# Adding three units' results to an SBUF residual with accumulating DMA transfers instead of VectorE

## The chip, the cores and the metric

The kernel runs on one core of a Trainium2 chip. Its time is the device time of one execution in microseconds; for the kernel before it is 1980.69 us, the median of two runs (1980.49 and 1980.89). A separate, profiled execution supplies the trace. All times inside the kernel are microseconds from the start of that trace's span, unless they are marked ns.

## The reference

One layer of an encoder block on 256 tokens of 2048 channels, all in float32:

```python
for l in range(DEPTH):                       # DEPTH = 1
    x = x + 0.5 * swiglu(rmsnorm(x, ffn1_norm[l]), ffn1_w_gate[l], ffn1_w_up[l], ffn1_w_down[l])
    h = rmsnorm(x, mix_norm[l])
    z = h @ w_in[l]                          # u, v and the gate logits
    ...                                      # a = pooling branch of u, b = convolution branch of v
    x = x + (g_a * a + g_b * b) @ w_out[l]
    x = x + 0.5 * swiglu(rmsnorm(x, ffn2_norm[l]), ffn2_w_gate[l], ffn2_w_up[l], ffn2_w_down[l])
return rmsnorm(x, final_norm)
```

`swiglu(h) = (silu(h @ w_gate) * (h @ w_up)) @ w_down` has a hidden width of 5632. The three assignments to `x` are the residual additions; the change concerns how they are carried out.

## The kernel before

**Tokens, units and chunks.** The 256 tokens are two token tiles of 128 partitions (t = 0, 1). The residual lies in SBUF for the whole run as two tiles `X[0]` and `X[1]`, 128 by 2048 float32 each. All weights stream from HBM once, as row tiles of 128 by 1024 float32 (512 KB). A *unit* is one product of the tokens with 1024 weight columns; a *chunk* is two row tiles of a unit. Each unit accumulates into one PSUM tile per token tile, `acc[t]`, of two banks of 512 columns. The pool of these tiles, `ps_a`, has three, so a new unit takes over the accumulators of the unit before it.

**The split.** Each row tile is turned into a rounded part `wh` (a cast on ScalarE, line 135) and a remainder `wl` (a subtraction on VectorE, line 137). Every product is three matmuls: high by high, high by low, low by high (line 208). The pool of split tiles holds two chunks, so the cast for a chunk waits until TensorE has finished the chunk two before it; five raw row tiles can be in SBUF, and SyncE issues a load when VectorE has finished with the tile in that place.

**The order of work.** The kernel is written out by hand: there is no scheduler, and each engine takes its instructions in the order in which the program emits them. For chunk i, `run` emits in this order: the load of a later chunk, the split of chunk i + 1, the functions that `at(i, ...)` has left for this place, and the matmuls of chunk i. When the last chunk of a unit has been emitted, the unit's `done` function follows. In that last chunk the matmuls of token tile 0 all come before those of token tile 1.

**What stands around the additions.** Five units add to the residual by the functions in question: the two halves of the first feed-forward's down product (`down_done`), the two halves of the mixer's output product (`wo_done`), and the first half of the second feed-forward's down product (`down_done` again). The second half of that last product ends in `final_tail`, which is not touched. With n for the last chunk of such a unit, each `done` does, for each token tile:

- two additions on VectorE, of 512 columns each, that read `acc` in PSUM and read and write `X` (line 301, with the factor 0.5; line 633 without one);
- `squares` (line 263): for each 512 columns of `X`, a ScalarE instruction with squared output and the row's sum, and one that reads the accumulator out.

For the first four of the five, `next_operand` then leaves work for later chunks. Before the matmuls of chunk n + 2, and again before those of n + 3, eight TensorE transposes read 512 columns of `X` (line 250; the first two groups q = 0, 1, then q = 2, 3). A group of four fills one of the two banks of `ps_t`, and ScalarE (line 241) and VectorE (line 242) turn it into the high and low part of the next product's operand. After a second half, `finish_rstd` is left for chunk n + 1: two small VectorE instructions on the sums of squares and a power on GpSimd (line 270).

The staging pool `stg` has two buffers for each tag; the tag `h` serves tiles of 128 by 512 float32. GpSimd's queue carries, besides that power, seven loads of broadcast rows (line 573).

Of the kernel before, what the change touches and what calls it, by code (L numbers as in the profile page):

```python
# [13 lines left out]
P = 128  # L14
# [20 lines left out]
WARM = 9  # L35
# after these row tiles of weights, the row tiles of x^T that are loaded
XT_LOADS = {(0, 0): (1, 2), (0, 1): (2, 4), (1, 0): (4, 8), (2, 0): (8, 12), (3, 0): (12, 16)}
TAPS = 6
TAPS_BUSY = 4

# columns of the packed per-partition vectors
V_N1, V_NM, V_N2 = 0, KD, 2 * KD
# [8 lines left out]
class Unit:  # L51
    """x[T, K*128] @ w[K*128, 1024]: K row tiles, two banks of 512 columns for each token tile."""

# [5 lines left out]
class Special:  # L59
    """A chunk of the weight stream with a use of its own."""  # L60

# [5 lines left out]
def encoder_kernel(ctx: ExitStack, tc: tile.TileContext, x, xT, vecs, rows, pool_m,  # L67
# [11 lines left out]

    # ---------------------------------------------------------------- constants and small state  # L80
    ident = const.tile([P, P], F32, name="ident")
# [10 lines left out]

    # ---------------------------------------------------------------- the stream of weight chunks
    stream = []
    side, middle = {}, {}

    def at(i, fn):
        """fn is emitted before the products of chunk i."""
        side.setdefault(i, []).append(fn)

    def amid(i, fn):
        """fn is emitted between the products of chunk i."""
        while isinstance(stream[i][0], Special):
            i += 1
        middle.setdefault(i, []).append(fn)
# [63 lines left out]
    def run_chunk(i):  # L169
        u, cc = stream[i]  # L170
        if isinstance(u, Special):
            u.use(split.pop(i))
            return
        if cc == 0:
            n = NT + 1 if u.tail else NT
            u.acc = [ps_a.tile([P, 2, C], F32, tag="acc", name=f"acc{i}_{t}") for t in range(n)]
        ws = split.pop(i)
        left = u.k // 2 - 1 - cc
        if u.tail and left < 2:
            # the last two chunks: token tile 0, then token tile 1 by columns  # L180
            for kk in range(2):
                products(u, 2 * cc + kk, 0, ws[kk])
            if left:
                u.kept = ws
                return
            u.tail(0, (0, 1), u.acc[0])
            for c in range(2):
                for kk in range(4):
                    products(u, 2 * cc - 2 + kk, 1, (u.kept + ws)[kk], (c,))
                u.tail(1, (c,), u.acc[1 + c])  # L190
            return
        order = [(kk, t) for kk in range(2) for t in range(NT)]
        if not left:
            order.sort(key=lambda o: o[1])
        for n, (kk, t) in enumerate(order):
            if n == 2:
                for fn in middle.pop(i, []):
                    fn()
            products(u, 2 * cc + kk, t, ws[kk])
        if not left:  # L200
            u.done(u.acc)
# [13 lines left out]

    # ---------------------------------------------------------------- operands of the products
    def pair(pool, tag, n, name):
        """hi and lo by row tile, four row tiles to a block."""
        r = []
        for b in range(n // 4):  # L220
            h, l = (block(pool, f"{tag}{s}{b}", F32R, f"{name}{s}{b}") for s in "hl")
            r += [(h[:, q, :], l[:, q, :]) for q in range(4)]
        return r
# [4 lines left out]
    def hidden(pool, name):  # L228
        """The feed-forward's hidden layer, hi and lo by row tile, four of them in a block."""
        return [tuple(block(pool, f"h{s}{u}", F32R, f"{name}{s}{u}") for s in "hl") for u in range(FF // C)]  # L230
# [7 lines left out]
    def scaled_split(dst, src, gain):  # L238
        """dst = hi and lo of src * gain, a scalar of each partition."""
        h, l = dst  # L240
        nc.scalar.activation(h, src, AF.Copy, scale=gain)
        nc.vector.scalar_tensor_tensor(out=l, in0=src, scalar=gain, in1=h.bitcast(F32),  # L242
                                       op0=ALU.mult, op1=ALU.subtract)

    def transposes(src_of, n, name):
        """n (up to 4 / NT) tiles [T, 128] into one bank as [128, T] each."""
        b = bank(name)
        for j in range(n):
            for t in range(NT):
                nc.tensor.transpose(out=b[:, j * T + t * P: j * T + (t + 1) * P],  # L250
                                    in_=src_of(j, t), identity=ident)
        return b

    def x_transposed(dst, gain_base, k0):
        """dst[k0], dst[k0 + 1] = the transposed residual times the gain."""
        b = transposes(lambda j, t: X[t][:, (k0 + j) * P:(k0 + j + 1) * P], 2, f"xt{Pos.now}_{k0}")
        for j in range(2):
            scaled_split(dst[k0 + j], b[:, j * T:(j + 1) * T], vcol(gain_base, k0 + j))

    def squares(t, slot, c0, c1):  # L260
        for n, c in enumerate(range(c0, c1, C)):
            junk = stg.tile([P, C], F32, tag="sg", name=f"sq{Pos.now}_{t}_{c}")
            nc.scalar.activation(junk, X[t][:, c:c + C], AF.Square,
                                 accum_out=ss[:, t, slot + n:slot + n + 1])

    def finish_rstd(dst):
        nc.vector.tensor_reduce(out=msq, in_=ss, axis=mybir.AxisListType.X, op=ALU.add)
        nc.vector.tensor_scalar(out=msq, in0=msq, scalar1=1.0 / D, scalar2=EPS,
                                op0=ALU.mult, op1=ALU.add)
        nc.gpsimd.tensor_tensor(dst, msq, mhalf, op=ALU.pow)  # L270

    # ---------------------------------------------------------------- feed-forward
    def ffn_units(w_g, w_d, xt, ht, rs, residual_done, tail=None):
# [22 lines left out]
        def down_done(half):  # L296
            def done(acc):
                for t in range(NT):
                    for c in range(2):
                        xs = X[t][:, half * W2 + c * C: half * W2 + (c + 1) * C]  # L300
                        nc.vector.scalar_tensor_tensor(out=xs, in0=acc[t][:, c, :], scalar=0.5, in1=xs,
                                                       op0=ALU.mult, op1=ALU.add)
                    squares(t, 2 * half, half * W2, (half + 1) * W2)
                residual_done(half)
            return done
# [6 lines left out]
    def next_operand(xt, gain_base, rs):  # L312
        """After each half of the residual: its transposed tiles, and in the end the row norms."""
        def f(half):
# [6 lines left out]

    # ---------------------------------------------------------------- pass 0: what starts the stream
    xt1 = pair(xtp, "x", KD, "xt1")
# [20 lines left out]

    # ---------------------------------------------------------------- plan
    def run(first, last):
# [9 lines left out]

    # phase 1
    ht_stack = ExitStack()
# [5 lines left out]

    # phase 2 units are appended before phase 1 runs, so that the weights run ahead
    mix = {}
# [62 lines left out]
    def ln_mean():  # L429
        """LayerNorm over the channels (partitions and tiles), spread over the chunks from here."""  # L430
        cv, cp = mix["conv"], conv_pairs()
# [93 lines left out]
    def use_pool_m(ws):  # L525
        """pooled^T = u^T M^T, M the window's sum less count times the token itself."""
        def group(g):
# [98 lines left out]
    def wo_done(half):  # L626
        def done(acc):
            if half == 0:
                xt3.extend(pair(xtp, "x", KD, "xt3"))
            for t in range(NT):  # L630
                for c in range(2):
                    xs = X[t][:, half * W2 + c * C: half * W2 + (c + 1) * C]
                    nc.vector.tensor_tensor(out=xs, in0=acc[t][:, c, :], in1=xs, op=ALU.add)
                squares(t, 2 * half, half * W2, (half + 1) * W2)
            next_operand(xt3, V_N2, rstd[2])(half)
# [18 lines left out]

    # phase 3 units
    ht2 = []
    fin = {}

    def final_tail(t, cs, acc):
        """The last of the residual, its norm and what is stored, for columns cs of token tile t."""  # L660
        pieces = [(c, 0, C) for c in cs] if t == 0 else [(c, a, T) for c in cs for a in (0, T)]
# [35 lines left out]

    # ---------------------------------------------------------------- run
    xr = [block(htp, f"h{s}{FF // C - 1 - j}", F32, f"xr{s}{j}") for j in range(2) for s in "hl"]
# [44 lines left out]
def _pack(w, cols):  # L744
    """[K*128, N] -> [units, K, 128, 1024]: cols[u] lists the column ranges of unit u."""
    import numpy as np
# [9 lines left out]
def _pool_constants():  # L756
    """M^T by window (tokens on partitions), and one over the counts."""
    import numpy as np
# [68 lines left out]
```

## Time and profile before

| what | value |
|---|---|
| median of the runs | 1980.69 us |
| span of the profiled execution, which is all that its record gives of its own time | 1978.6 us |
| runs' median less that span | 2.1 us |
| TensorE busy (matmul rows) | 1966.4 us, 99% |
| VectorE busy | 1110.4 us, 56% |
| ScalarE busy | 874.5 us, 44% |
| GpSimd busy | 11.0 us, 1% |
| mean granted TensorE clock | 0.999 |
| VectorE additions at line 301 / line 633 | 12 / 8 |

A busy share is a mean over stages. The view of chains follows the work that ended last back to what released each step; the timeline gives the instructions of a stretch in order of time, neighbours of one kind merged, with an idle time in brackets and what ended it.

### The profile page before, as it was taken

What the parts mean: (1) busy time and instruction counts of PE and PEld (TensorE: products, weight loads), DVE (VectorE), ACT (ScalarE), POOL (GpSimd) and SP (SyncE); (2) the same over time, 40 slices, a digit from 0 to 9 for tenths busy, and PEclk for the clock granted to TensorE, in tenths of its full rate; (3) what the DMA queues carried; (4) which work ended last, traced back from release to release, by engine and by line L of the source; (5) the groups of instructions that cost most, each with busy time, mean ns of one, the idle gap of its engine ahead of it and who ended that gap; (6) DMA issues with size and microseconds to landing.
All of it is one profiled execution on the core that took longest, in us unless ns stands there. A gap on an engine that the chain in (4) does not pass through costs nothing.

```text
span 1978.6 us, 22916 instructions
## 1 busy us (share of the span) xinstructions
PE 1966.4 (99%) x8848; PEld 1629.5 (82%) x8848; DVE 1110.4 (56%) x1224; ACT 874.5 (44%) x997; POOL 11.0 (1%) x22
## 2 busy tenths in 40 slices
PE   9999999999999999999999999999999999999998
PEld 7888888888888888888888888888888888888886
DVE  5454544444445445888897765555544444444444
ACT  6444444444434345454444544544444444443433
POOL 0000000000000000000000000000000000000000
PEclk9999999999999999999999999999999999999999
DMA  8555555555555656666666555555555555565564
GB/s 310 193 188 196 190 192 188 187 189 190 192 191 187 195 189 202 194 195 211 202 208 205 184 185 185 181 186 198 191 188 189 189 190 192 181 198 195 192 192 149
DMA packets 106141, 383.88 MB, mean 194 GB/s; under 512 B 11920, under 2 KB 12176, under 8 KB 105776
## 3 DMA queue, kind: packets, MB, share of 16 engines
q1 hardware_dynamic: 104688, 378.45, 58.4%
q0 software_dynamic: 1056, 3.83, 0.6%
q8 instruction: 69, 1.13, 0.2%
q14 instruction: 40, 0.33, 0.1%
q10 hardware_dynamic: 288, 0.14, 0.0%
HBM read 380.28 MB, written 2.10 MB: 193 GB/s over the span
## 4 chain that ended last, share of the span: by engine, by line
PE 99%; DMA 1%; issue 0%; ACT 0%; DVE 0%; DVEq 0%; POOLq 0%; POOL 0%; ACTq 0%
PE acc L208 96%; PE hT L250 1%; PE xt L250 0%; DMA raw<-in_w_g 0%; PE mixb L560 0%; DMA xrh<-in_xT 0%; PE pool L535 0%; PE mT L250 0%; PE gT L250 0%; ACT fsq L668 0%; ACT wh L135 0%; PE ln_mean L442 0%; PE ln_var L471 0%; DVE X L680 0%; DVE X L665 0%
## 5 line engine op out<-in xcount | busy, mean ns | idle before, releaser
L137 DVE TENSOR_TENSOR wl<-raw,wh 128x1024 fp32r<-128x1024 f32 (+1 forms) x706 | 853.8, 1221 | 741.7 <-ACT wh L135 741.5
L135 ACT CAST wh<-raw 128x1024 fp32r<-128x1024 f32 (+1 forms) x706 | 736.2, 1050 | 906.9 <-PE acc L208 849.6
L208 PE MATMUL acc<-wh,xt1h 128*128 128x512 f32 x704 | 219.2, 392 | 1.8 <-ACT wh L135 0.9
L208 PE MATMUL acc<-wh,xt3h 128*128 128x512 f32 x704 | 218.9, 392 | 0.0
L208 PE MATMUL acc<-wl,xt1h 128*128 128x512 f32 x704 | 217.4, 390 | 0.1
L208 PE MATMUL acc<-wl,xt3h 128*128 128x512 f32 x704 | 217.1, 390 | 0.0
L208 PE MATMUL acc<-wh,xt1l 128*128 128x512 f32 x704 | 216.9, 389 | 0.0
L208 PE MATMUL acc<-wh,xt3l 128*128 128x512 f32 x704 | 216.8, 389 | 0.0
L208 PEld LDWEIGHTS acc<-wl,xt1h 128*128 128x128 f32 x704 | 132.1, 188 | 28.1 <-DVE wl L137 0.4
L208 PEld LDWEIGHTS acc<-wh,xt1l 128*128 128x128 f32 x704 | 132.1, 188 | 28.2 <-DVE xt1l L242 0.5
L208 PEld LDWEIGHTS acc<-wh,xt3l 128*128 128x128 f32 x704 | 132.1, 188 | 27.8
L208 PEld LDWEIGHTS acc<-wl,xt3h 128*128 128x128 f32 x704 | 132.1, 188 | 27.8
L208 PEld LDWEIGHTS acc<-wh,xt1h 128*128 128x128 f32 x704 | 130.6, 188 | 28.6 <-ACT wh L135 1.5
L208 PEld LDWEIGHTS acc<-wh,xt3h 128*128 128x128 f32 x704 | 130.5, 188 | 25.8
L208 PE MATMUL acc<-wh,xt2h 128*128 128x512 f32 x448 | 138.3, 390 | 0.0
L208 PE MATMUL acc<-wl,xt2h 128*128 128x512 f32 x448 | 138.1, 389 | 0.0
L208 PE MATMUL acc<-wh,xt2l 128*128 128x512 f32 x448 | 138.0, 389 | 0.0
L208 PE MATMUL acc<-wh,ht2h 128*128 128x512 f32 x352 | 109.2, 390 | 0.0
L208 PE MATMUL acc<-wl,ht2h 128*128 128x512 f32 x352 | 109.1, 389 | 0.0
L208 PE MATMUL acc<-wh,ht2l 128*128 128x512 f32 x352 | 109.0, 389 | 0.0
L208 PE MATMUL acc<-wh,ht1h 128*128 128x512 f32 x352 | 108.7, 390 | 0.0
L208 PE MATMUL acc<-wh,ht1l 128*128 128x512 f32 x352 | 108.4, 389 | 0.0
(144 smaller groups left out, 1699.9 us busy)
## 6 DMA issues: line engine op xcount, KB each, us to landing
raw<-in_w_g SPq DMA_DIRECT2D x350, 512.0 KB, 3.3
raw<-in_w_d SPq DMA_DIRECT2D x176, 512.0 KB, 3.5
raw<-in_w_in SPq DMA_DIRECT2D x112, 512.0 KB, 4.2
raw<-in_w_out SPq DMA_DIRECT2D x32, 512.0 KB, 4.2
raw<-in_w_pp SPq DMA_DIRECT2D x16, 512.0 KB, 4.0
raw<-in_w_cp SPq DMA_DIRECT2D x16, 512.0 KB, 4.0
row<-in_rows POOLq DMA_DIRECT2D x7, 512.0 KB, 4.2
X<-in_x SPq DMA_DIRECT2D x2, 1024.0 KB, 8.9
```

The lines of the kernel that those rows point to most:

```text
L135: nc.scalar.copy(out=h, in_=src)
L137: nc.vector.tensor_tensor(out=l, in0=src, in1=h.bitcast(F32), op=ALU.subtract)
L208: nc.tensor.matmul(u.acc[t + c if u.tail and t else t][:, c, :], lhsT=a, rhs=b[:, c * C:(c + 1) * C], start=k == 0 and n == 0, stop=k == u ...
L250: nc.tensor.transpose(out=b[:, j * T + t * P: j * T + (t + 1) * P], in_=src_of(j, t), identity=ident)
```

## The change

The VectorE additions of the five units become a copy on ScalarE and a DMA transfer. For each 512 columns, ScalarE reads the accumulator from PSUM, multiplies it by 0.5 or 1.0 and writes a staging tile `part` in SBUF (tag `h`); GpSimd's queue issues a transfer that adds `part` to the columns of `X` in SBUF. `squares` moves from the end of chunk n to chunk n + 1, behind the casts of chunk n + 2; the transposes stay where they were. Comments are dropped elsewhere in the file without effect.

```diff
+    def add_to_residual(t, half, acc, by):
+
+        for c in range(2):
+            part = stg.tile([P, C], F32, tag="h", name=f"part{Pos.now}_{t}_{c}")
+            nc.scalar.activation(part, acc[:, c, :], AF.Copy, scale=by)
+            nc.gpsimd.dma_start(out=X[t][:, half * W2 + c * C: half * W2 + (c + 1) * C], in_=part,
+                                accum_op=ALU.add)
+
...
         def down_done(half):
             def done(acc):
                 for t in range(NT):
-                    for c in range(2):
-                        xs = X[t][:, half * W2 + c * C: half * W2 + (c + 1) * C]
-                        nc.vector.scalar_tensor_tensor(out=xs, in0=acc[t][:, c, :], scalar=0.5, in1=xs,
-                                                       op0=ALU.mult, op1=ALU.add)
-                    squares(t, 2 * half, half * W2, (half + 1) * W2)
+                    add_to_residual(t, half, acc[t], 0.5)
+                n = Pos.now
+                at(n + 1, lambda: [squares(t, 2 * half, half * W2, (half + 1) * W2) for t in range(NT)])
                 residual_done(half)
...
             for t in range(NT):
-                for c in range(2):
-                    xs = X[t][:, half * W2 + c * C: half * W2 + (c + 1) * C]
-                    nc.vector.tensor_tensor(out=xs, in0=acc[t][:, c, :], in1=xs, op=ALU.add)
-                squares(t, 2 * half, half * W2, (half + 1) * W2)
+                add_to_residual(t, half, acc[t], 1.0)
+            n = Pos.now
+            at(n + 1, lambda: [squares(t, 2 * half, half * W2, (half + 1) * W2) for t in range(NT)])
             next_operand(xt3, V_N2, rstd[2])(half)
```

## The prediction

> **What bounds the kernel now.** I read the page first: the busy shares, the chain and the granted clock, with the wait that fills ScalarE's idle time below them.
>
> ```profile
> PE 1966.4 (99%) x8848; PEld 1629.5 (82%) x8848; DVE 1110.4 (56%) x1224; ACT 874.5 (44%) x997; POOL 11.0 (1%) x22
> PE 99%; DMA 1%; issue 0%; ACT 0%; DVE 0%; DVEq 0%; POOLq 0%; POOL 0%; ACTq 0%
> core 0: 1978.6 us, clock 0.999
> ACT wh L135 <- PE acc L208: 849.6, 520, 3.0
> ```
>
> TensorE is busy for 1966.4 of 1978.6 us at a granted clock of 0.999, the chain is TensorE for 99%, and ScalarE spends 849.6 us waiting for TensorE to give split buffers back. So nothing saved on VectorE can show, unless TensorE waits for it. All that the change could give back is in what TensorE loses now, 12.2 us, and the stretches (length, then each engine's busy time, TensorE first) put 11.6 of these outside the five units:
>
> ```profile
> 0.00:10.00 10.00, 7.92 (x32) 6.58 (x33) 3.54 (x7) 5.08 (x9) 0.78 (x8) 1.00 0.80 277
> 10.00:20.00 10.00, 9.07 (x39) 6.86 (x38) 7.46 (x9) 6.37 (x10) 0.00 (x0) 1.00 1.03 413
> 1968.00:1978.00 10.00, 1.42 (x7) 0.84 (x5) 3.69 (x9) 3.62 (x11) 0.56 (x1) 0.83 0.62 211
> ```
>
> What the change can cost is any new TensorE wait, and TensorE never makes up for one.
>
> Next comes the timeline around the first of the five units (n is its last chunk).
>
> ```profile
> 614.83 1.29 DVE L301 SCALAR_TENSOR_TENSOR X<-acc,X 128x512 f32<-128x512 f32 x2 [0.41 <-PE acc L208]
> 615.55 0.63 ACT L263 ACTIVATE sq<-X 128x512 f32<-128x512 f32 x1 [2.39 <-DVE X L301]
> 617.55 1.29 DVE L301 SCALAR_TENSOR_TENSOR X<-acc,X 128x512 f32<-128x512 f32 x2 [1.43 <-PE acc L208]
> 619.58 2.93 ACT L135 CAST wh<-raw 128x1024 fp32r<-128x1024 f32 x3
> 622.56 1.02 PEld L250 LDWEIGHTS xt<-ident,X 128*128 128x128 f32 x8
> 622.99 1.05 ACT L135 CAST wh<-raw 128x1024 fp32r<-128x1024 f32 x1 [0.47 <-PE acc L208]
> 620.65 4.65 DVE L137 TENSOR_TENSOR wl<-raw,wh 128x1024 fp32r<-128x1024 f32 x4 [1.81 <-ACT wh L135]
> 627.66 0.48 DVE L242 SCALAR_TENSOR_TENSOR xt2l<-xt,vec,xt2h 128x256 fp32r<-128x256 f32 x1 [0.55 <-ACT xt2h L241]
> 629.15 1.03 PE L250 MATMUL xt<-ident,X 128*128 128x128 f32 x8
> ```
>
> I count from 614.83, when token tile 0's accumulator is complete: token tile 1's follows at 2.72, the transposes that begin chunk n + 2 load `X` at 7.73, and those of n + 3 run at 14.32. The additions end at 4.01, 3.7 us ahead of their reader: that is the room into which the new path must fit. The other three units with transposes have the same spacing:
>
> ```profile
> 736.35 1.29 DVE L301 SCALAR_TENSOR_TENSOR X<-acc,X 128x512 f32<-128x512 f32 x2 [0.41 <-PE acc L208]
> 744.31 1.03 PE L250 MATMUL xt<-ident,X 128*128 128x128 f32 x8
> 1190.88 1.29 DVE L633 TENSOR_TENSOR X<-acc,X 128x512 f32<-128x512 f32 x2 [0.41 <-PE acc L208]
> 1198.84 1.03 PE L250 MATMUL xt<-ident,X 128*128 128x128 f32 x8
> 1236.24 1.29 DVE L633 TENSOR_TENSOR X<-acc,X 128x512 f32<-128x512 f32 x2 [0.41 <-PE acc L208]
> 1244.20 1.03 PE L250 MATMUL xt<-ident,X 128*128 128x128 f32 x8
> ```
>
> The transposes' matmuls follow by 7.96 us each time (622.79 - 614.83 in the first unit, 0.23 behind the load).
>
> **The change part by part.** The prices on the engines:
>
> ```profile
> L301 DVE SCALAR_TENSOR_TENSOR X<-acc,X 128x512 f32<-128x512 f32 x12 | 7.7, 686 | 5.5 <-PE acc L208 5.5
> L633 DVE TENSOR_TENSOR X<-acc,X 128x512 f32<-128x512 f32 x8 | 5.2, 686 | 3.7 <-PE acc L208 3.7
> L135 ACT CAST ht1h<-hT 128x512 fp32r<-128x512 f32 x22 | 12.8, 581 | 0.0
> L263 ACT ACTIVATION_READ_ACCUMULATOR sq<-X 128x1 f32 x28 | 5.2, 186 | 0.0
> L573 POOL DMA_DIRECT2D row<-in_rows x7 | 3.7, 537 | 1004.7 <-PE acc L208 694.7 <-DVE pooled L539 165.6 <-DVE gate L581 144.4
> ```
>
> *Removed:* 20 additions of 686 ns, 13.7 us of VectorE. At each of them VectorE had been idle before (5.5 + 3.7 us in all), so this is worth nothing in the total.
>
> *Added on ScalarE:* 20 copies from PSUM. The nearest row is the cast of 128x512 from PSUM, 0.58 us; I take 0.59 with the hand-over, 12 us in all. ScalarE stood idle for 2.39 us before the first square, so the first copy starts at 0.0. *Added on GpSimd:* 20 issues at 0.54 us, 10.7 us on an engine busy for 11. Behind them on its queue stand, in the second unit, two row loads, and after each second half the power of `finish_rstd`. The loads slip from 739.34 by about 3 us, and their first reader (VectorE) comes at 892.2; the power's result is read at the end of a whole unit, so both stay hidden:
>
> ```profile
> 739.34 1.06 POOL L573 DMA_DIRECT2D row<-in_rows  x2 [694.69 <-PE acc L208]
> L539 DVE TENSOR_TENSOR pooled<-pool,row x4: 682/682/683, 892.2 to 911.1; 128x512 f32<-128x512 f32 x4
> ```
>
>
> *The new wait:* `part` uses tag `h` with two buffers. The third copy of a unit (token tile 1, first 512 columns) may overwrite the first `part` only when the first transfer has landed. Let L be the time from a transfer's issue to its landing. The four copies c0 to c3 and their transfers then run:
>
> - c0 ends at 0.59, its transfer lands at 0.59 + L; c1 ends at 1.18, lands at 1.18 + L;
> - c2 starts at 0.59 + L (for L above 2.13), ends at 1.18 + L, and its transfer lands at 1.18 + 2L;
> - c3 ends at 1.77 + L and lands at 1.77 + 2L.
>
> So L counts twice. In ScalarE's queue behind c2 and c3 stand the two casts of chunk n + 2 (1.77 + L to 3.87 + L; TensorE needs the first after the transposes, at 7.73 + 1.02 = 8.75), so these are late only beyond any wait of the transposes themselves.
>
> **First stall, S1.** The first transposes of chunk n + 2 read c2's columns: S1 = 1.18 + 2L - 7.73 = 2L - 6.55.
>
> **Second stall, S2.** The squares now stand behind the casts of n + 2 and wait for the last transfers; at 0.63 + 0.19 each they end at 2.80 + 2L. Behind them in the same queue are the casts of n + 3 (to 4.90 + 2L), then the operand pieces out of the banks. VectorE's second `wl` ends at 6.3 + 2L, and from there to the last piece the old trace takes 628.14 - 625.30 = 2.84, so the second bank comes free at about 9.2 + 2L. Chunk n + 3's second group of transposes needs it at 14.1 + 0.5 + S1 = 8.05 + 2L. Hence S2 = 1.1 us, whatever L is above 3.3. In the old order there were 1.3 us of room here.
>
> **The fifth unit** has no transposes, but its successor takes three accumulators, and its third is the one that c2 and c3 still read:
>
> ```profile
> 1849.68 1.29 DVE L301 SCALAR_TENSOR_TENSOR X<-acc,X 128x512 f32<-128x512 f32 x2 [1.43 <-PE acc L208]
> 1850.84 0.68 PE L208 MATMUL acc<-wh,ht2h 128*128 128x512 f32 x2
>   PEld acc L208: 0.2, 1
> ```
>
> TensorE's weight load already waits 0.2 us there for the additions, which end at 4.01 in this unit's count; c3 ends at 1.77 + L, so TensorE stands L - 2.24 longer.
>
> Total: 4 x (2L - 6.55 + 1.1) + (L - 2.24) = 9L - 24.0 us.
>
> **L itself.** No transfer in this trace adds, and none goes from SBUF to SBUF. The nearest rows:
>
> ```profile
> row<-in_rows POOLq DMA_DIRECT2D x7, 512.0 KB, 4.2
> X<-in_x SPq DMA_DIRECT2D x2, 1024.0 KB, 8.9
> out_y<-X SPq DMA_DIRECT2D x8, 256.0 KB, 2.9
> vec<-in_vecs POOLq DMA_DIRECT2D x1, 156.0 KB, 2.7
> DMA to landing us min/median/max: 3.8/4.2/5.3
> q1 hardware_dynamic: 104688, 378.45, 58.4%
> ```
>
> The last two rows are the spread of the row loads and the weights' share of the DMA engines. A transfer of the change writes 256 KB but has to read the columns of `X` as well as `part`, 512 KB in. From below, 2.7 us: less than the 156 KB that GpSimd's queue brought. From above, 8.9 us: the 1 MB load amid the crowded start. I take 4.2, GpSimd's own 512 KB row, beside the same weight traffic. The sum is 9 x 4.2 - 24.0 = 13.8 us, made of four times (1.85 + 1.1) and 1.96. The profiled execution's 1978.6 becomes 1992.4, and with the 2.1 us by which the median of the runs lies above it, 1994.5 us. At the slowest row, 5.3, it is 23.7 us.
>
> The Trainium skill (DMA: Bandwidth & Descriptors, "Anatomy of one DMA — SWDGE (gpsimd) path") fits a transfer of GpSimd's queue as 2.0 us plus bytes over 436 GB/s, an estimate of 2.6 us for 256 KB. By it the row loads should take 3.2 us and the trace has 4.2. The skill (Collectives: The Full Stack, "The bandwidth ceiling: the fold count and why AG ≠ RS ≠ AR") also says that an add in the DMA path costs two source reads and not the arithmetic; no run here shows that yet.
>
> *Other queues.* SyncE issues weight loads when `wl` is done; `wl` of n + 3 ends some 4 us later than before. Five buffers at one row tile per 2.72 us (half a chunk) span 13.6 us; a load of 512 KB takes about 4.2 of them, cast and subtraction 1.05 + 4.65 / 4 = 2.2, so 7 us are cover. If that were gone, each further microsecond would stall TensorE one to one.
>
> **The rivals.**
>
> *Hidden.* L is 3.0 us or less, nearer to `vec` and the 256 KB stores. At 2.7 S1 is gone, S2 (then 2L - 5.4) too, and the fifth unit costs 0.5: 1981 us. For it: a transfer inside SBUF has no HBM to wait for. Against it: twice the reading. The skill's fit named above gives this case. Chance 0.22.
>
> *Slow adding, on the other side.* If an adding transfer costs its engines several times a copy, row by row, L passes 7.07, where 9L - 24.0 reaches 2% (39.6 us). At the 8.9 of the 1 MB row it is 56 us: 2037. TensorE would then stand 11 us at a time, and the clock row speaks against getting off with that:
>
> ```profile
> 1974.00:1975.00 1.00, 0.00 (x0) 0.00 (x0) 0.00 (x0) 0.00 (x0) 0.00 (x0) 0.76 1.07 379
> 1975.00:1976.00 1.00, 0.00 (x0) 0.00 (x0) 0.00 (x0) 0.00 (x0) 0.00 (x0) 0.50 1.07 344
> ```
>
> Some 5 us after the last matmul the granted clock falls from 1.00 to 0.50 (third figure from the right). Stalls of 1.85 us are far from that, stalls beyond 5 us would pay again. The Trainium skill (TensorE: Matmul & The Clock Gate, "Part 1: The HAM clock gate") says the same of pauses over about 3.4 us. Chance of this case 0.13.
>
> *Not what it says.* Were the transfers put off or doing nothing, or VectorE's relief worth something, the time would be 1979 to 1981. Chance 0.02; TensorE's 99% allows no more.
>
> **How the numbers follow.** The forecast (L from 3.0 to 7.0, 1983 to 2020) has 0.63. The range goes from 1981 (hidden) to 2016 (L of 6.6) and leaves out less than 2 in 10, nearly all above. A measurement of this kernel can tell about 2% from no change: slower by that 0.13, faster 0.01, within 0.86.
>
> **What would show it.** The rows at line 301 and 633 vanish, and ScalarE gets 20 copies near 0.59 us. The transposes' weight loads wait for a DMA four times, by about 1.9 us, and again for VectorE's operand pieces by about 1.1; c2 waits about 1 us for a landing. The landing time of the adding transfers is the number on which all hangs: under 3 I am too high, above 6 too low. I would be wrong in kind if TensorE waited for casts of `wh` or for weight loads, or if the transfers slowed the weights' queue.

## The result and the profile after

The changed kernel takes 2000.16 us (median of 2 runs, 1998.32 to 2002.00) against 1980.69: a ratio of 1.0097, with a 95% interval from 1.0068 to 1.0127. Four later runs beside new runs of the kernel before give 1.0102 (1.0085 to 1.0119). The forecast was 1994.5 us, with a range from 1981 to 2016; 13.8 us of loss were forecast, 19.5 came.

The page of the changed kernel, busy times and the chain by engine and by line:

```profile
PE 1974.6 (99%) x8848; PEld 1634.2 (82%) x8848; DVE 1097.8 (55%) x1204; ACT 884.4 (44%) x1017; POOL 26.7 (1%) x42
PE 95%; DMA 2%; issue 1%; ACT 1%; DVE 1%; POOL 0%; ACTq 0%; DVEq 0%; POOLq 0%
```

VectorE gave up 12.6 us, ScalarE took 9.9, and TensorE is no longer the whole chain. TensorE lost in two ways: its idle time went from 12.2 to 25.6 us (span less busy time), and for the same 8848 instructions it was busy 8.2 us longer. The second was not in my sum. The waits, with total us, times and the longest:

```profile
ACT part L270 <- DMA X<-part: 20.0, 9, 5.2
PEld xt L250 <- DMA X<-part: 7.1, 4, 2.6
PEld acc L208 <- ACT part L270: 2.7, 1, 2.7
PE xt L250 <- DVE xt2l L242: 1.7, 2, 0.8
```

All the stalls of the prediction are here: the third copy of a unit waits for the first landing, the transposes wait for the third transfer (S1), the product of the fifth unit waits for the accumulator, and later transposes wait for the operand pieces on VectorE (S2; most of it stands under other releasers in this view). The prices, in the same order of views as before (the copies, GpSimd's issues, the size and the median landing, the spread of landings):

```profile
L270 ACT ACTIVATE part<-acc x20: 593/598/600, 615.1 to 1870.3; 128x512 f32<-128x512 f32 x20
L271 POOL DMA_DIRECT2D X<-part x20 | 17.5, 953 | 1459.1 <-ACT part L270 815.6 <-PE acc L208 643.5
X<-part POOLq DMA_DIRECT2D x20, 256.0 KB, 3.7
DMA to landing us min/median/max: 3.3/3.7/6.1
```

The timeline of the first unit, to be laid beside that of the kernel before (counted from 615.11):

```profile
615.11 1.09 ACT L270 ACTIVATE part<-acc 128x512 f32<-128x512 f32 x2 [1.67 <-PE acc L208]
616.02 1.77 POOL L271 DMA_DIRECT2D X<-part  x2 [571.05 <-ACT part L270]
619.65 0.60 ACT L270 ACTIVATE part<-acc 128x512 f32<-128x512 f32 x1 [3.46 <-DMA X<-part]
621.11 0.60 ACT L270 ACTIVATE part<-acc 128x512 f32<-128x512 f32 x1 [0.86 <-DMA X<-part]
623.49 0.63 ACT L263 ACTIVATE sq<-X 128x512 f32<-128x512 f32 x1
623.92 0.75 PEld L250 LDWEIGHTS xt<-ident,X 128*128 128x128 f32 x7 [0.94 <-DMA X<-part]
626.16 1.98 ACT L135 CAST wh<-raw 128x1024 fp32r<-128x1024 f32 x2
631.08 0.42 PEld L250 LDWEIGHTS xt<-ident,X 128*128 128x128 f32 x4 [1.14 <-PE acc L208]
632.54 0.42 PEld L250 LDWEIGHTS xt<-ident,X 128*128 128x128 f32 x4 [1.04 <-PE xt L250]
```

The third copy waits 3.46 us, the loads of the first transposes 0.94 us, and those of the second group, before chunk n + 3, wait twice, 1.14 and 1.04 us. The other three units with transposes show the same waits, with other lengths. The start of a unit's first copy, against that of its first addition before, tells what each unit cost; the first unit's stands above, the other four are:

```profile
739.38 1.09 ACT L270 ACTIVATE part<-acc 128x512 f32<-128x512 f32 x2 [1.67 <-PE acc L208]
1200.07 1.09 ACT L270 ACTIVATE part<-acc 128x512 f32<-128x512 f32 x2 [1.67 <-PE acc L208]
1249.08 1.09 ACT L270 ACTIVATE part<-acc 128x512 f32<-128x512 f32 x2 [1.67 <-PE acc L208]
1864.41 1.09 ACT L270 ACTIVATE part<-acc 128x512 f32<-128x512 f32 x2 [1.67 <-PE acc L208]
```

In the kernel before, the first additions of the other four units stand in the prediction, and that of the fifth is here:

```profile
1846.96 1.29 DVE L301 SCALAR_TENSOR_TENSOR X<-acc,X 128x512 f32<-128x512 f32 x2 [0.41 <-PE acc L208]
```

The first unit starts 0.28 us later than before, the second 3.03, the third 9.19, the fourth 12.84, the fifth 17.45, and the span ends 21.6 later. The differences are the units' costs: 2.75, 6.16, 3.65, 4.61 and 4.15 us, where 2.95 four times and 1.96 were forecast. The largest excess sits in the second, fourth and fifth units, and there the granted clock has a part in it. The stretches (length, busy time of TensorE first; the granted clock is the third figure from the right):

```profile
755.84:759.25 3.41, 1.19 (x9) 1.01 (x10) 1.88 (x5) 2.54 (x5) 0.00 (x0) 1.00 1.01 392
759.25:762.66 3.41, 3.41 (x10) 2.66 (x9) 2.87 (x4) 1.86 (x4) 0.00 (x0) 0.50 0.51 177
1206.40:1209.80 3.40, 2.03 (x10) 1.40 (x10) 1.50 (x2) 3.07 (x6) 1.61 (x2) 1.00 0.63 107
1209.80:1213.20 3.40, 3.40 (x19) 2.95 (x20) 0.96 (x2) 3.06 (x9) 0.00 (x0) 1.00 0.96 251
1257.59:1261.00 3.41, 1.40 (x10) 1.32 (x11) 2.36 (x2) 3.41 (x8) 0.84 (x1) 1.00 1.03 177
1261.00:1264.41 3.41, 3.41 (x10) 2.66 (x9) 1.68 (x4) 2.99 (x6) 0.71 (x1) 0.50 0.74 279
1868.59:1872.00 3.41, 1.15 (x6) 0.88 (x6) 0.14 (x1) 2.30 (x4) 1.69 (x2) 1.00 0.62 106
1872.00:1875.41 3.41, 3.41 (x10) 2.64 (x9) 2.22 (x2) 3.14 (x8) 0.05 (x1) 0.50 1.01 217
```

Three times the clock is 0.50 for 3.41 us, after a stretch of that length in which TensorE was busy for 1.15 to 1.40 us; the third unit left 2.03 us busy and kept its clock. A fall takes away 3.41 x 0.5 = 1.7 us, three of them 5.1. Without them the five units cost 21.3 - 5.1 = 16.2 us. A fourth fall, at 8.34 us, lies in the start of the kernel, ahead of all units; the first unit starts only 0.28 us later than before, so it has no share in these costs.

### The profile page after: what moved, and what is told of

Its sections match the earlier page's. It is cut to its first block, busy times and chain, and to the rows that moved or that the text cites. A ratio compares the mean times of both kernels' runs of the same rounds, so it can differ in the third digit from the quotient of the medians.

```text
span 2000.2 us, 22962 instructions
## 1 busy us (share of the span) xinstructions
PE 1974.6 (99%) x8848; PEld 1634.2 (82%) x8848; DVE 1097.8 (55%) x1204; ACT 884.4 (44%) x1017; POOL 26.7 (1%) x42
## 3 DMA queue, kind: packets, MB, share of 16 engines
q0 software_dynamic: 3936, 9.07, 2.1%
## 4 chain that ended last, share of the span: by engine, by line
PE 95%; DMA 2%; issue 1%; ACT 1%; DVE 1%; POOL 0%; ACTq 0%; DVEq 0%; POOLq 0%
PE acc L208 93%; DMA X<-part 2%; PE hT L250 1%; DVE wl L137 0%; PE mixb L566 0%; POOL X L271 0%; ACT wh L135 0%; ACT part L270 0%; DMA xrh<-in_xT 0%; PE pool L541 0%; DVE xt2l L242 0%; DVE xt3l L242 0%; PE mT L250 0%; PE xt L250 0%; ACT xt3h L241 0%
```

## The experiments

My theory after the comparison has three parts: the landing counts twice because two staging buffers make the third copy wait (S1), the squares in ScalarE's queue carry the last landing on to the next operand (S2), and the pauses cost clock when they fill more than half of a fixed time window. The rivals: the transfers are slow through contention or through the adding itself; the clock goes by the length of one pause. The table gives what each unit cost in each kernel's profile, in the way just shown.

| kernel | unit 1 | 2 | 3 | 4 | 5 | median of runs, us |
|---|---|---|---|---|---|---|
| the change | 2.75 | 6.16 | 3.65 | 4.61 | 4.15 | 2000.16 |
| four staging buffers | 3.85 | 2.39 | 2.53 | 2.74 | -0.05 | 1992.39 |
| squares late | 0.64 | 1.63 | 0.83 | 1.71 | 2.48 | 1990.60 |
| both | 0.00 | 0.00 | 0.24 | 0.69 | -0.05 | 1980.93 |
| transposes late | 0.61 | 1.61 | 0.55 | 1.33 | 4.23 | 1989.70 |
| copying instead of adding | 1.03 | 2.17 | 1.23 | 3.11 | 0.99 | 1989.01 |
| the fifth unit alone | 0.00 | 0.01 | 0.00 | 0.00 | 4.17 | 1984.58 |
| squares moved alone | 0.00 | 0.01 | 0.00 | 0.00 | 0.05 | 1980.51 |

The kernel before had medians of 1980.44 to 1980.66 us beside these.

**Squares moved alone.** The kernel before, with its VectorE additions, and the squares where the change puts them:

```diff
-                    squares(t, 2 * half, half * W2, (half + 1) * W2)
+                n = Pos.now
+                at(n + 1, lambda: [squares(t, 2 * half, half * W2, (half + 1) * W2) for t in range(NT)])
                 residual_done(half)
...
```

The mixer's units have the same edit.

> The kernel before, additions on VectorE, with only the squares moved to chunk n + 1 behind the casts, as the change has them. Theory: the additions end at 4.0 us, the squares by 7.0 us, the casts of chunk n + 3 are on time: 1980 to 1981.5 us, no stall. Rival (the place of the squares alone makes the second stall): 1984 us or more.

Measured: 1980.51 us, ratio 1.0001 (0.9991 to 1.0010). The place of the squares costs nothing by itself; the runs below show that it costs when the data they wait for is late.

**Four staging buffers.**

```diff
-            part = stg.tile([P, C], F32, tag="h", name=f"part{Pos.now}_{t}_{c}")
+            part = stg.tile([P, C], F32, tag="part", bufs=4, name=f"part{Pos.now}_{t}_{c}")
```

> Four staging buffers of their own for the parts instead of two under tag h, nothing else. Double-landing theory (the third copy waits for the first landing, so a landing time counts twice): that wait goes, the third copy starts at 2.7 us after token tile 0's accumulator is complete, its transfer lands at 7.0 to 8.0 against 7.73 at which the transposes read; the first stall shrinks from 0.9 to 2.6 us to 0 to 0.4 in each of four units, the fifth unit's stall goes, the second stall (squares in front of the casts) stays at about 0.9 us each, and the granted clock no longer falls: 1984 to 1986 us. Rival (the transfers are slow because they share the DMA engines with the weight loads and with each other): landing times grow to 5 us and more when four are in flight, the first stall stays at 1 us or more: 1989 us or more.

Measured: 1992.39 us (ratio 1.0062, 1.0047 to 1.0077), well above 1984 to 1986. S1 and the fifth unit's stall went as expected. S2 did not stay at 0.9; it took S1's place. The timeline of its first unit, which begins at 615.07:

```profile
622.81 1.02 PEld L250 LDWEIGHTS xt<-ident,X 128*128 128x128 f32 x8
625.04 0.63 ACT L263 ACTIVATE sq<-X 128x512 f32<-128x512 f32 x1 [1.69 <-DMA X<-part]
630.58 0.42 PEld L250 LDWEIGHTS xt<-ident,X 128*128 128x128 f32 x4 [1.45 <-issue]
632.05 0.42 PEld L250 LDWEIGHTS xt<-ident,X 128*128 128x128 f32 x4 [1.04 <-PE xt L250]
```

The first transposes run at once, but the last square waits until 625.04 for the fourth landing, and so starts almost as late as in the change (625.53). So S2 hangs on the moment at which ScalarE is through with the squares, and S1 merely hid part of it. The rival's part is that with four transfers in flight beside the weight loads the median landing grew from 3.7 to 4.4 us. The clock did not stay up either: the two pauses of the first unit's second group, of 1.06 and 0.83 us of TensorE, fall into one stretch of 3.41 us, and the next stretch ran at 0.50, which is in the 3.85 us of this unit.

```profile
629.33:632.74 3.41, 1.52 (x10) 1.11 (x10) 1.88 (x5) 2.64 (x5) 0.00 (x0) 1.00 0.80 276
632.74:636.15 3.41, 3.41 (x9) 2.63 (x8) 2.87 (x5) 1.77 (x4) 0.00 (x0) 0.50 0.45 137
```

**Squares late**, with two buffers:

```diff
-                at(n + 1, lambda: [squares(t, 2 * half, half * W2, (half + 1) * W2) for t in range(NT)])
+                for t in range(NT):
+                    at(n + 4 + t, lambda t=t: squares(t, 2 * half, half * W2, (half + 1) * W2))
...
-                at(n + 1, lambda: finish_rstd(rs))
+                at(n + 6, lambda: finish_rstd(rs))
...
```

The mixer's units have the first edit as well.

> The change, but the squares stand in chunks n + 4 and n + 5 and the row norm in n + 6. Theory: only the second stall goes (measured 0.3 to 2.5 us in each of four units), with the one fall of the clock that follows it; the first stalls (7.1 us together), the fifth unit's 2.4 us and two falls of the clock at 1.7 us stay: 1992 to 1995 us. Rival (the squares do no harm; the second stall comes from the late transposes themselves): 1998 to 2002 us as the change.

Measured: 1990.60 us, runs from 1987.70 to 1991.50, ratio 1.0047 (1.0032 to 1.0062). The profiled run is the one of 1987.70, without any fall of the clock, and behind the start its waits are almost S1 and the fifth unit alone:

```profile
PEld xt L250 <- DMA X<-part: 5.4, 4, 1.8
PEld acc L208 <- ACT part L270: 2.6, 1, 2.6
```

So S2 is the squares' doing; that S1 is the double landing's, the four buffers showed. The median lies 1.4 us below what I expected.

**Both.**

> Both: four staging buffers and the squares in chunks n + 4 and n + 5. Theory: every named stall goes but 0 to 0.4 us of the first in each unit: 1980.5 to 1982.5 us. Rival (VectorE's relief is worth something): below 1980 us. Rival (contention with the weight loads): 1985 us or more.

Measured: 1980.93 us, ratio 1.0002 (0.9992 to 1.0011). What is left of the stalls is one row, under a microsecond at a time:

```profile
PEld xt L250 <- DMA X<-part: 1.2, 2, 0.9
```

With these two edits the accumulating transfers are as good as VectorE's additions and no better: 12.6 us less of VectorE are worth nothing that shows here, as forecast. The landings had even grown, to a median of 5.0 us and at most 7.1; they cost next to nothing, because only two groups of transposes still wait for them.

**Transposes late.**

```diff
-                at(n + 2 + q // 2, lambda q=q: x_transposed(xt, gain_base, 8 * half + 2 * q))
+                at(n + 3 + q // 2, lambda q=q: x_transposed(xt, gain_base, 8 * half + 2 * q))
```

> The change, but the transposes stand before chunks n + 3 and n + 4 instead of n + 2 and n + 3; two staging buffers, squares as in the change. Theory: both stalls of the four units go, since the reader comes 5.4 us later; the fifth unit keeps its 2.4 us and its fall of the clock (1.7 us) or not: 1983 to 1985 us. Rival (ScalarE, held by the wait on the landing, is late with the casts): 1988 us or more, with TensorE waiting for the split tiles.

Measured: 1989.70 us (ratio 1.0048, 1.0031 to 1.0065), almost 5 us above what I expected. S1 is gone, but the rival holds: ScalarE, held by the third copy, casts chunk n + 2 late, and without S1 as a cover the product waits for the split tile.

```profile
PEld acc L208 <- DVE wl L137: 3.1, 5, 1.0
PEld acc L208 <- ACT part L270: 2.8, 1, 2.8
```

Units 1 to 4 still cost 4.1 us together, the fifth 4.2 with a fall of the clock (1859.88 to 1863.29). Of the 9.4 us of the profile's span another 1.1 lie ahead of the first unit, and I have no cause for them.

**Copying instead of adding.** The same kernel as the change, without `accum_op`; it leaves out the residual addition:

```diff
-            nc.gpsimd.dma_start(out=X[t][:, half * W2 + c * C: half * W2 + (c + 1) * C], in_=part,
-                                accum_op=ALU.add)
+            nc.gpsimd.dma_start(out=X[t][:, half * W2 + c * C: half * W2 + (c + 1) * C], in_=part)
```

> The transfers copy part over the columns of X instead of adding to them, so the addition of the residual is left out. The price of the adding by itself: if it costs a second read only, the landing falls from 3.4 us (second transfer of a unit) and 3.6 to 5.4 us (first) by 0.3 to 1 us, GpSimd's issue from 0.87 to about 0.55 us, and the time by 4 to 10 us. If the adding in the DMA path is slow by itself, the landing falls to 2.5 us or less and the time to 1985 us or less. If it costs nothing, all stays as in the change.

Measured: 1989.01 us (one run), 11 us less than the change:

```profile
L271 POOL DMA_DIRECT2D X<-part x20 | 10.8, 543 | 1457.1 <-ACT part L270 813.3 <-PE acc L208 643.4
X<-part POOLq DMA_DIRECT2D x20, 256.0 KB, 2.8
DMA to landing us min/median/max: 2.3/2.8/5.1
```

The adding costs 0.9 us of landing, of which a third is GpSimd's longer issue (typically 0.87 against 0.54 us). GpSimd's queue also has 64 packets fewer per transfer (2656 in all, for 3936 in the change). That fits a second read rather than an adder that is slow by itself, without proving it. The Trainium skill says the same of an add in the DMA path: it costs a second source read, not cycles of the adder (Collectives: The Full Stack, "The bandwidth ceiling: the fold count and why AG ≠ RS ≠ AR"). The Trainium skill's fit for a transfer of GpSimd's queue (DMA: Bandwidth & Descriptors, "Anatomy of one DMA — SWDGE (gpsimd) path"), 2.6 us by my estimate, is close to the copy's 2.8 and does not hold for the adding transfer's 3.7. No fall of the clock came in this profile. Of the 13.0 us between the two profiles' spans (2000.2 and 1987.2) the three falls are therefore at most 5.1, and the shorter landings have the rest.

**The fifth unit alone** (the four others add on VectorE as before).

> Only the fifth unit (the first half of the second feed-forward's down product) adds by transfers; the other four are as before. Theory: its stall at the third accumulator (2.4 us) and at most one fall of the clock (1.7 us): 1983 to 1985 us. Rival (the stalls of a unit only shift work that is made up later): 1980.7 us.

Measured: 1984.58 us, ratio 1.0019 (1.0009 to 1.0029). The ten runs fall into two groups: 1982.92 and 1982.99, one at 1983.84, and seven from 1984.39 to 1985.36. The profiled run, one of the slower, has the fifth unit's wait as in the change (2.7 us) and then the fall of the clock:

```profile
1851.40:1854.80 3.40, 1.11 (x5) 0.62 (x4) 0.00 (x0) 1.79 (x3) 1.16 (x2) 1.00 0.56 96
1854.80:1858.20 3.40, 3.40 (x9) 2.64 (x8) 2.36 (x2) 3.13 (x8) 0.56 (x1) 0.50 1.01 179
```

**Doses of stalls.** In the kernel before, for 20 chunks of the first feed-forward, a small matmul between the chunk's halves waits for a chain of k GpSimd writes that starts when TensorE enters the chunk:

```diff
...
+        def begin():
+            b = bank(f"tick{i}")
+            nc.tensor.matmul(b[:, :2], lhsT=ones, rhs=ones[:, :2], start=True, stop=True)
+            nc.scalar.copy(out=tick, in_=b[:, :2])
+            nc.gpsimd.tensor_tensor(tock, tick, mhalf, op=ALU.pow)
+            for _ in range(k):
+                nc.gpsimd.memset(hold, 1.0)
...
+            nc.tensor.matmul(b[:, :P], lhsT=ones, rhs=hold[:, :P], start=True, stop=True)
...
+    for j in range(20):
+        stall(12 + 4 * j, 3 + j)
```

> The kernel before with 20 artificial pauses of TensorE of growing length (0 to about 5 us) in the first feed-forward, four chunks apart: between the two halves of a chunk a small matmul waits for a chain of GpSimd writes. Window theory: the granted clock is decided on a fixed grid of 3.41 us, and falls to half for one window when more than about half of the window before was idle: pauses under 1.7 us never cost clock, pauses of 1.7 to 3.4 us do or do not, by where they lie on the grid, and pauses over about 3.4 us always do. Rival (a fixed length of one pause decides): a sharp limit in the length, wherever it lies on the grid.

Measured: pauses from 1.03 to 8.56 us. Every fall behind a pause begins on one grid of 3.413 us (all 18 starts within 0.1 us of it). Two pauses on either side of the limit, each with its stretch of the grid and the next:

```profile
103.31 0.49 PE L379 MATMUL hold<-hold,ones 128*128 128x128 f32 x2 [1.93 <-POOL hold L375]
101.12:104.53 3.41, 1.48 (x8) 1.08 (x7) 2.59 (x3) 1.04 (x1) 1.91 (x5) 1.00 0.65 175
104.53:107.95 3.42, 3.42 (x10) 2.52 (x10) 0.00 (x0) 0.00 (x0) 0.00 (x0) 0.51 0.79 280
130.13 0.49 PE L379 MATMUL hold<-hold,ones 128*128 128x128 f32 x2 [1.72 <-POOL hold L375]
128.42:131.83 3.41, 1.70 (x8) 1.46 (x9) 1.23 (x1) 1.04 (x1) 1.43 (x5) 1.00 0.49 163
131.83:135.25 3.42, 3.42 (x16) 2.82 (x15) 0.74 (x1) 1.05 (x1) 0.00 (x0) 1.00 0.41 144
```

A pause of 1.93 us that lies in one window halves the clock of the next, one of 1.72 us does not. In this run the limit is between 1.48 and 1.70 us of work in a window of 3.41. Every pause in this kernel from 1.93 us up was followed by a fall, because each happened to put over 1.9 us into some window; so this run by itself shows the grid and the limit, but no pause of over 1.9 us that the grid spared. By itself it would fit the rival too, with a limit in the length between 1.72 and 1.93 us. Two other profiles decide against that. With four staging buffers two pauses of 1.06 and 0.83 us in one window cost clock. And with the squares late, the fifth unit's pause of 2.22 us lies across two windows, and the clock stays:

```profile
1858.27 0.50 PE L208 MATMUL acc<-wh,ht2h 128*128 128x512 f32 x1 [2.22 <-ACT part L270]
1856.50:1859.91 3.41, 1.64 (x7) 1.38 (x8) 0.73 (x1) 2.59 (x4) 1.74 (x2) 1.00 0.62 105
1859.91:1863.32 3.41, 3.41 (x17) 2.83 (x16) 2.77 (x3) 2.00 (x3) 0.00 (x0) 1.00 0.96 231
```

Taken together, the limit lies between about 1.5 and 1.64 us of work. The Trainium skill (TensorE: Matmul & The Clock Gate, "Part 1: The HAM clock gate") gives the same free-running window of 3413 ns, but lets the clock fall "after ≥1 idle window"; these rows differ, for the windows ahead of a fall were busy for up to 1.52 us.

**The change again**, for the spread:

> The change itself, more runs. Window theory: the stalls without the clock are the same each time (about 16 us over the kernel before, 1996.5 us), and each run adds 1.7 us for every grid window that the stalls happen to leave more than half idle, by where the grid lies: single runs at 1996 to 2004 us, a spread over ten times that of the kernel before, median 1998 to 2002. In the profile every fall lasts 3.41 us and follows a window with over 1.7 us idle. Rival (the stalls themselves vary with the landing times): the spread goes with the sum of the waits, not with the count of falls.

Measured: 2000.05 to 2002.79 us, median 2001.39; ratio 1.0102. Its profile has two falls in the units, in 2 and 5, where the first had three, and yet nearly the same span (2000.4): unit 4 kept its clock and cost 4.17 us, against 4.61 with a fall. There the half-speed chunk had hidden S2. So a fall is worth less than 1.7 us where a later wait would have come anyway, and the expected constant 16 us beside the clock does not hold: without the falls the units cost 16.2 us in one profile and 18.0 in the other. The rival has a part in the spread.

**The fifth unit, with its wait filled.** Five small matmuls into an unread bank stand ahead of the waiting product:

```diff
+            if u.tail and cc == 0 and n == 1:
+                fill = bank("fill")
+                for _ in range(5):
+                    nc.tensor.matmul(fill[:, :P], lhsT=ones, rhs=ones, start=True, stop=True)
             products(u, 2 * cc + kk, t, ws[kk])
```

> The kernel in which only the fifth unit adds by transfers (its runs lie at 1983 or at 1984 to 1985), and five small matmuls into an unread bank, about 1.2 us, stand in TensorE's queue just before the product that waits for the third accumulator. Window theory: the wait itself stays (the product is released at the same moment), but only about 1.1 us of it is idle, no grid window is over half idle, and the clock never falls: all runs near 1983, median 1982.5 to 1983.3, against 1984.6 without the filling. Rival (the fall of the clock is not decided by how much of a window is idle): the same two groups of runs, median 1984 to 1986.

Measured: median 1983.41 us, 1.2 below the unfilled kernel and just above the 1983.3 that I had allowed. Seven of ten runs are at 1982.70 to 1983.57, three at 1984.18 to 1985.63. In the profile (1982.76 us) the product is released after 1.21 us of idleness instead of 2.3, and the clock stays at 1.00:

```profile
1853.35 0.50 PE L212 MATMUL acc<-wh,ht2h 128*128 128x512 f32 x1 [1.21 <-ACT part L274]
```

The groups have swapped sizes as the window theory wants, but ten runs a kernel cannot make that certain: against the kernel before, the intervals of the two (1.0006 to 1.0026 here, 1.0009 to 1.0029 unfilled) overlap. The three slow runs the theory did not foresee; they have no profile, and whether a longer landing made their pause longer stays open.

## Why the prediction was right, and where it was off

**The bound.** TensorE sets the time, VectorE's 13.7 us were worth nothing that shows: the kernel with four buffers and late squares is without them, and is as fast as the kernel before (1.0002, 0.9992 to 1.0011).

**The copies and the other queues.** Forecast 0.59 us, measured 0.598. GpSimd's issues were 0.87 us and not 0.54; the accumulating kind costs more, and no row of before could show it. Nothing stood behind them that mattered, and behind the start no product stood for its weights longer than 0.4 us.

**The landing, counted twice.** I took L = 4.2. In the first unit the first transfer takes 3.95 us from the end of its copy to the start of the third copy (619.65 - 615.70), the third 3.67 from the end of its copy to the transposes (623.92 - 620.25), 7.6 in all for 2L = 8.4. The other units come to 8.5, 8.4 and 9.3, the last of them here:

```profile
1255.38 0.60 ACT L270 ACTIVATE part<-acc 128x512 f32<-128x512 f32 x1 [5.21 <-DMA X<-part]
1259.60 0.74 PEld L250 LDWEIGHTS xt<-ident,X 128*128 128x128 f32 x7 [2.64 <-DMA X<-part]
```

The mean of the four is 8.45. S1 was forecast at 7.4 us over four units and measured at 7.1 by the waits of the weight loads. That 4.2 fitted so well was partly luck: from issue to landing the median is 3.7, and the rest is the first transfers' longer landings (3.5 to 5.3 us) and some 0.3 us between the end of a copy and its issue (615.70 to 616.02), which stood at nothing in the sum. The spread from unit to unit is almost all in the first transfer. My sign that the third copy would wait about 1 us did not follow from my own sum: there it starts at 0.59 + 4.2 = 4.79, 2.1 us behind the accumulator at 2.72; it started at 4.54.

**The second stall** was undersized: 4.4 us forecast; before the second group of transposes TensorE stood 1.6, 2.5, 1.7 and 0.3 us, 6.1 in all. The delay is larger than the idle time: with TensorE's 8848 instructions laid side by side with those of the kernel before, in order, the products behind these transposes come 2.0, 2.9, 2.1 and 0.5 us later than those ahead of them, 7.4 in all. The fourth is small because the half-speed chunk ahead of it hid it; in the second profile of the change, where unit 4 kept its clock, the four are 2.0, 2.9, 2.2 and 2.2. So 1.1 us a unit was about half of what it costs. I had the fourth copy start 0.59 us behind the third. It starts 1.46 behind (621.11 - 619.65), because the second landing follows the first by GpSimd's longer issue and more, and all that ScalarE has queued moves with it; the difference of 0.87 us is about what the first unit's 2.0 has above 1.1. In units 2 to 4 the last square waited for its landing besides.

**The fifth unit**: 1.96 us forecast, 2.45 measured without the clock (4.15 - 1.7), for the same reason: its fourth copy ends 6.5 us after the unit's start and not 1.77 + 4.2 = 6.0.

**The clock** is the step that failed in kind. I wrote that stalls of 1.85 us are far from costing clock, from one row: after the last matmul the clock held for some 5 us. What that row showed was a grid, not a delay: 3.41 us windows, of which the last busy one and the first idle one had still to end. The five units cost 21.3 us in the profile, 7.5 above the forecast 13.8. By the same comparison of products the three falls delay them by 4.8 us, S2 by 3.0 more than forecast, the fifth unit by 0.5 more and S1 by 0.9 less (6.5 for 7.4): 7.4 of the 7.5. The share of the clock changes from run to run: in the second profile two falls have 3.2 us, and S2, not hidden in unit 4, has more.

**The rivals.** Hidden transfers did not come true with the change's own order; they do with two edits, though with longer landings (median 5.0 us), not with the 3.0 or less that this rival asked for. The slow adding did not either: in the change no landing took over 6.1 us, and the total stayed under 2%.

## What to carry to other kernels

Before an addition is moved from an engine to a transfer, count how often the landing stands in a row before the next reader: here the count, set by the staging buffers and by what waits in the same in-order queue, decided between 20 us lost and nothing. An unread result that only feeds a statistic belongs behind the work that the bound engine needs next. And when the bound engine gets several short waits, sum them within a clock window: two pauses that are harmless apart can cost clock together, as 1.06 and 0.83 us did with four buffers.

## What the runs showed of the hardware that was not expected

- In the middle of these kernels the granted TensorE clock fell to 0.50 for the next 3.41 us window when TensorE was busy for 1.52 us or less of a window at full clock; with 1.64 us or more it stayed. At the start of the kernel that limit does not hold: in the change a window from 4.93 us with 2.14 us busy was followed by a fall. The windows lie on a fixed grid, so that a pause of 2.22 us kept the clock (squares late) and one of 1.93 us lost it (doses of stalls).
- An accumulating transfer of 256 KB inside SBUF lands 3.3 to 6.1 us after its issue (median 3.7, the profile of the change) beside a stream of weights, a copy 2.3 to 5.1 (2.8). GpSimd needs 0.87 us to issue the one, 0.54 the other.
